# Latent attention on one Trainium2 core: keys and values of two head groups projected ahead of the first queries, a later transposition of probabilities, and shorter weight tiles

## The chip, the cores and the metric

The kernel runs on one core of a Trainium2 chip, as one launch. The metric is the device time of an execution in microseconds, as the median of several runs. TensorE is written PE here, VectorE DVE, ScalarE ACT, GpSimd POOL and SyncE SP.

## What is computed

The reference runs two blocks of two layers each on one sequence of 256 tokens with 1024 features. The first block mixes by forgetting attention, a short convolution and pooling, then by a gated feed-forward layer. In the second block the first layer mixes by latent attention and the second by dilated attention, each followed by a feed-forward layer. The change is in the latent attention, and in numbers that all parts share:

```python
def mla_mixer(h, pos, w_in, g_qa, w_qb, g_kva, w_kvb, g_q, g_k, w_o):
    proj = h @ w_in
    q_lat = proj[..., :Q_LORA]                      # 384
    kv_lat = proj[..., Q_LORA:Q_LORA + KV_LORA]     # 256
    k_rope = rope(proj[..., Q_LORA + KV_LORA:], pos)
    q = (rms_norm(q_lat, g_qa) @ w_qb).reshape(B, S, MLA_HEADS, MLA_QK)
    kv = (rms_norm(kv_lat, g_kva) @ w_kvb).reshape(B, S, MLA_HEADS, MLA_NOPE + MLA_V)
    ...
    q = rms_norm(q, g_q)
    k = rms_norm(k, g_k)
    o = dense_attention(q, k, v, MLA_QK ** -0.5)    # 16 heads, softmax over all 256 keys
    return o.reshape(B, S, MLA_HEADS * MLA_V) @ w_o
```

## The kernel before, in words

**Weights.** `plan()` writes a list of weight chunks in the order of their use. `use(ci)` (from L318) returns the chunk whose turn it is; it starts the DMA of a chunk four ahead into a `raw` tile (SP's queue, L304) and the split of a chunk two ahead. Float32 products are built from two reduced-precision parts: ACT casts the weights to `whi` (L313) and DVE subtracts to get `wlo` (L314). `mm3` then issues three matmuls for one product: L362 to L364 where the weights move through PE, L366 to L368 where they are held. A chunk has at most 2048 floats a partition; `CHUNK` sets only how long the tiles are.

**Order.** The code issues work in program order, and a scheduler (the Tile framework's) decides from it, from its own costs and from free buffers the order on each engine. An engine runs its list strictly in that order. So a row that waits holds up everything below it.

**Latent attention.** The 16 heads are four groups g of four. `lat_proj` and `latent` (L1268 to L1298) make the latents of keys and of queries, normalise them (DVE L1288), transpose them on PE (L1294) and split them for the next product (ACT L474, DVE L475). For a group there are three pieces:

- `proj_kv(g)` (L1319): 12 matmuls of 512 columns into two accumulator banks, then ACT's square (L1330), DVE's sum (L1331) and a copy of the values (L1337). Called kv0 to kv3 below.
- `post_kv(g)` (L1341): DVE writes the scaled keys out of the same two banks (L1345, L1346). Only then are the banks free.
- `proj_q(g)` (L1350): 18 matmuls of 384 columns into two banks, ACT's square (L1360) and copy (L1361), DVE's sum (L1362) and the rotation (L1255 to L1258), which reads the banks too. Called q0 to q3.

There are four accumulator banks in PSUM (`accp`), used by every product, and four other PSUM banks (`attp`) for scores and transposes. `tr_qk(hd)` transposes a head's queries and keys (PE L1374, ACT L1376 and L1377).

`attn_std` (L650) runs the heads as a pipeline: scores of head i (`st0`: PE L674, DVE L677 and L678, ACT's exponential L640, DVE L643 and L648), then the transposition of the probabilities of head i - D1 (`st1`: PE L695, ACT L697), then, for a pair of heads, the product with the values of heads i - D2 (`st2`: PE L707 and L711, split by ACT L479 and DVE L480). `D1, D2` are 3 and 6 for the first block's causal attention and 1 and 4 here. Probabilities and their transposes take tiles of 512 floats from one pool, `t2p`, of five.

A table of due steps calls kv2, q2, kv3, q3 and the heads' `tr_qk` between the heads. From step 23 on, `out_ahead` fills in matmuls of the output projection (L366 to L368), whose weights are split like all others. Beside all that run pieces of the bias of the dilated attention (PE L760 and L762, DVE L744, L769 and L775), fed in by `next(bias)`.

The start of the attention, before:

```python
    proj_kv(0)
    qlT = next(qlT)
    proj_q(0)
    post_kv(0)
    proj_kv(1)
    proj_q(1)
    post_kv(1)
    for hd in range(4):
        tr_qk(hd)
```

`next(qlT)` is the transposition of the latent queries.

Of the kernel before, what the change touches and what calls it, by code (L numbers as in the profile page):

```python
# [55 lines left out]

CHUNK = 2112
LOWP = 100  # L60


def seq_chunks(blocks):

    return [("blk", blocks[i:i + 16]) for i in range(0, len(blocks), 16)]


def plan():
    chunks = []
# [37 lines left out]
        chunks.append(("wide", "mla_w_in_2", 0, k0, 4, [(384, 288)]))  # L107
    for k0 in (0, 4):
        chunks.append(("wide", "mla_w_in_2", 0, k0, 4, [(0, 384)]))
    for g in range(4):  # L110
        kn = [((4 * g + h) * 128, 64) for h in range(4)]
        vv = [((4 * g + h) * 128 + 64, 64) for h in range(4)]
        chunks.append(("wide", "mla_w_kvb_2", 0, 0, 2, kn + vv))
        chunks.append(("wide", "mla_w_qb_2", 0, 0, 3, [(g * 384, 384)]))
    chunks += seq_chunks([("mla_w_o_2", 0, k * 128, m * 128) for m in range(8) for k in range(8)])
    for i in range(2):
        if i == 1:
# [123 lines left out]
def tile_net(ctx, tc, wts, ada, xin, cols_in, table_in, fb_in, c_in, pos_in, inv_in, mask_in, freq_in, out):  # L241
# [6 lines left out]
    rawp = ctx.enter_context(tc.tile_pool(name="rawp", bufs=4))  # L248
    splp = ctx.enter_context(tc.tile_pool(name="splp", bufs=3))
    t1p = ctx.enter_context(tc.tile_pool(name="t1p", bufs=6))  # L250
    t2p = ctx.enter_context(tc.tile_pool(name="t2p", bufs=5))
    smp = ctx.enter_context(tc.tile_pool(name="smp", bufs=14))
    accp = ctx.enter_context(tc.tile_pool(name="accp", bufs=4, space=PS))
    attp = ctx.enter_context(tc.tile_pool(name="attp", bufs=4, space=PS))
# [34 lines left out]


    chunks = plan()
    offs, o = [], 0
    for c in chunks:
# [7 lines left out]
    def w_dma(ci):  # L301
        n = chunk_size(chunks[ci])
        r = mk(rawp, [128, CHUNK], F32, "raw")
        nc.sync.dma_start(out=r[:, :n], in_=wts[offs[ci]:offs[ci] + 128 * n].rearrange("(p f) -> p f", f=n))  # L304
        raw[ci] = r

    def split_piece():
        ci, a, b, last = pend.pop(0)
        if a == 0:
            spl[ci] = (mk(splp, [128, CHUNK], F32R, "whi"), mk(splp, [128, CHUNK], F32R, "wlo"))  # L310
        hi, lo = spl[ci]
# [203 lines left out]
    for _ in range(12):  # L515
        PE.matmul(out=wps[:, :128], lhsT=ones, rhs=ones, start=True, stop=True)
    raw[0] = mk(rawp, [128, CHUNK], F32, "raw")
    w0 = wts[0:128 * 1056].rearrange("(p f) -> p f", f=1056)
# [131 lines left out]
    def attn_std(heads, qkT, vcol, oT, causal, qscale=None, done=set()):  # L650


        P, PT, O = {}, {}, {}
        D1, D2 = (3, 6) if causal else (1, 4)

        def st0(h_):
            qk = qkT(h_)
# [661 lines left out]
    def proj_kv(g):  # L1319
        w = use(nextc())  # L1320
        akv = [acc(), acc()]
        for k in range(2):
            for tt in range(2):
                mm3(akv[tt], w, slice(k * 512, k * 512 + 512), parts(kvT[k], slice(tt * 128, tt * 128 + 128)), k == 0, k == 1, wmov=True, ns=648)
        vt = bt([128, 2, 256])
        vM[g] = vt
        ss = sm(8)
        for tt in range(2):
            sq = t1()
            S.activation(out=sq, in_=akv[tt][:, :256], func=AF.Square)  # L1330
            V.tensor_reduce(out=ss[:, 4 * tt:4 * tt + 4], in_=sq.rearrange("p (a b) -> p a b", a=4), axis=AX.X, op=ALU.add)  # L1331
        V.tensor_tensor(out=ss[:, :8].rearrange("p (t a) -> p t a", t=2), in0=ss[:, :8].rearrange("p (t a) -> p t a", t=2),
                        in1=skr.unsqueeze(2).to_broadcast([128, 2, 4]), op=ALU.add)
        r = sm(8)
        rsqrt_small(r[:, :8], ss[:, :8], 8, 1.0 / 96)
        for tt in range(2):
            S.copy(out=vt[:, tt, :], in_=akv[tt][:, 256:512])  # L1337
        postM[g, 1] = (akv, r)

    def post_kv(g):  # L1340
        akv, r = postM.pop((g, 1))  # L1341
        for tt in range(2):
            rk = r[:, 4 * tt:4 * tt + 4].unsqueeze(2)
            ka = bt([128, 4, 96])
            V.tensor_tensor(out=ka[:, :, 0:64], in0=akv[tt][:, :256].rearrange("p (a b) -> p a b", a=4), in1=rk.to_broadcast([128, 4, 64]), op=ALU.mult)  # L1345
            V.tensor_tensor(out=ka[:, :, 64:96], in0=kr[tt].to_broadcast([128, 4, 32]), in1=rk.to_broadcast([128, 4, 32]), op=ALU.mult)  # L1346
            qaM[g, 1, tt] = ka

    def proj_q(g):
        w = use(nextc())  # L1350
        aq = [acc(), acc()]
        for k in range(3):
            for tt in range(2):
                mm3(aq[tt][:, :384], w, slice(k * 384, k * 384 + 384), parts(qlT[k], slice(tt * 128, tt * 128 + 128)), k == 0, k == 2, wmov=True, ns=490)
        ss = sm(8)
        for tt in range(2):
            qb = bt([128, 4, 96])
            q3 = aq[tt][:, :384].rearrange("p (a b) -> p a b", a=4)
            sq2 = t2()
            S.activation(out=sq2[:, :384], in_=aq[tt][:, :384], func=AF.Square)  # L1360
            S.copy(out=qb[:, :, 0:64], in_=q3[:, :, 0:64])  # L1361
            V.tensor_reduce(out=ss[:, 4 * tt:4 * tt + 4], in_=sq2[:, :384].rearrange("p (a b) -> p a b", a=4), axis=AX.X, op=ALU.add)  # L1362
            rope_to(qb[:, :, 64:96], q3[:, :, 64:96], tt, t1([128, 4, 32]), 4)
            qaM[g, 0, tt] = qb
        r = mk(smp, [128, 8], F32, "rq", 3)
        rsqrt_small(r, ss[:, :8], 8, 1.0 / 96)
        rM[g] = r
# [46 lines left out]
        yield acs  # L1414

    proj_kv(0)
    qlT = next(qlT)
    proj_q(0)
    post_kv(0)
    proj_kv(1)  # L1420
    proj_q(1)
    post_kv(1)
    for hd in range(4):
# [242 lines left out]
```

## Time and profile before

| | |
|---|---|
| median of 3 runs | 1575.88 us (1573.53 to 1576.39) |
| the profiled execution's own time | 1574.72 us |
| its span, first to last instruction | 1573.0 us |
| mean granted clock of PE | 0.999 of full speed |
| busy: PE, DVE, ACT, POOL | 1551.7, 1188.2, 899.7, 227.3 us |
| read from HBM | 311.32 MB, 203 GB/s over the span |

The times in the trace are in microseconds from the start of the span. Busy time of PE is the union of its matmuls; the weight loads (PEld) lie beside them. In a timeline a row gives start, duration, engine, line of the kernel, operation, output and inputs, and in brackets how long the engine stood idle before it and what released it. Durations of neighbouring rows overlap a little, since engines are pipelined.

### The profile page before, as it was taken

Reading aid. Unit: us, or ns where it says so; the run is one execution under the profiler, and the core shown is the slowest. Engines: PE = TensorE matmul, PEld = TensorE weight load, DVE = VectorE, ACT = ScalarE, POOL = GpSimd, SP = SyncE. Lnnn points to the kernel's source line nnn. Section 1 sums busy time; section 2 is a strip of 40 time slices with the busy share of each in tenths; the row PEclk is TensorE's granted clock in tenths of the full one; section 3 lists DMA queues with packets and bytes.
Section 4 is the critical chain, followed back from the end, with each engine's and each line's share of the span. In section 5 each row is a group of like instructions: output and inputs, shape, how many; then the busy total and the mean of one; then the engine's idle time right before and its main releaser. Section 6 shows DMA issues by size and latency. Waiting matters only on the chain.

```text
span 1573.0 us, 31268 instructions
## 1 busy us (share of the span) xinstructions
PE 1551.7 (99%) x12314; PEld 1506.7 (96%) x12314; DVE 1188.2 (76%) x2430; ACT 899.7 (57%) x1854; POOL 227.3 (14%) x273
## 2 busy tenths in 40 slices
PE   8999999999999999999999999999999999999999
PEld 7999999999899999999987899999999999999999
DVE  7877877789787777778788688767777777686642
ACT  7574554433557454443258677533676766677632
POOL 1100100055210010004332100010223222110000
PEclk9999999999999999999999999999999999999999
DMA  8455666645655666664435267776666767655551
GB/s 315 168 188 201 218 240 218 238 170 163 214 195 189 229 222 228 219 241 170 140 116 188 87 238 265 266 284 224 218 218 210 221 199 236 202 200 186 191 198 41
DMA packets 83907, 320.69 MB, mean 204 GB/s; under 512 B 31984, under 2 KB 34816, under 8 KB 58928
## 3 DMA queue, kind: packets, MB, share of 16 engines
q1 hardware_dynamic: 83184, 317.30, 59.0%
q8 instruction: 97, 1.59, 0.4%
q0 software_dynamic: 432, 1.28, 0.3%
q14 instruction: 50, 0.41, 0.1%
q10 hardware_dynamic: 144, 0.11, 0.0%
HBM read 311.32 MB, written 7.34 MB: 203 GB/s over the span
## 4 chain that ended last, share of the span: by engine, by line
PE 91%; DVE 5%; ACT 1%; issue 1%; POOL 1%; DMA 1%; SPq 0%; ACTq 0%; DVEq 0%; POOLq 0%
PE acc L366 22%; PE acc L368 21%; PE acc L367 21%; PE acc L362 6%; PE acc L363 6%; PE acc L364 6%; DVE wlo L314 2%; PE att L760 1%; PE att L1548 1%; POOL sm L405 1%; PE att L1550 1%; PE att L1562 1%; PE acc L707 1%; PE att L674 1%; PE att L1579 1%
## 5 line engine op out<-in xcount | busy, mean ns | idle before, releaser
L314 DVE TENSOR_TENSOR wlo<-raw,whi 128x1024 fp32r<-128x1024 f32 (+2 forms) x508 | 582.6, 1165 | 149.5 <-ACT whi L313 148.5
L313 ACT CAST whi<-raw 128x1024 fp32r<-128x1024 f32 (+2 forms) x508 | 495.5, 1000 | 313.2 <-PE acc L367 187.4
L366 PE MATMUL acc<-b,whi 128*128 128x256 f32 x1744 | 498.5, 286 | 2.3 <-ACT b L479 0.9
L367 PE MATMUL acc<-b,whi 128*128 128x256 f32 x1744 | 490.0, 281 | 0.0
L368 PE MATMUL acc<-b,wlo 128*128 128x256 f32 x1744 | 489.2, 281 | 0.0
L366 PE MATMUL acc<-h,whi 128*128 128x256 f32 (+1 forms) x1216 | 343.1, 282 | 0.8 <-DVE t L1102 0.8
L368 PE MATMUL acc<-h,wlo 128*128 128x256 f32 (+1 forms) x1216 | 342.2, 281 | 0.0
L367 PE MATMUL acc<-h,whi 128*128 128x256 f32 (+1 forms) x1216 | 341.3, 281 | 0.0
L366 PEld LDWEIGHTS acc<-b,whi 128*128 128x128 f32 x1744 | 328.1, 188 | 6.3 <-issue 3.2
L367 PEld LDWEIGHTS acc<-b,whi 128*128 128x128 f32 x1744 | 328.5, 188 | 1.2 <-issue 0.8
L368 PEld LDWEIGHTS acc<-b,wlo 128*128 128x128 f32 x1744 | 328.5, 188 | 0.1
L366 PEld LDWEIGHTS acc<-h,whi 128*128 128x128 f32 x1216 | 229.8, 189 | 0.9 <-issue 0.9
L368 PEld LDWEIGHTS acc<-h,wlo 128*128 128x128 f32 x1216 | 229.1, 188 | 0.0
L367 PEld LDWEIGHTS acc<-h,whi 128*128 128x128 f32 x1216 | 229.0, 188 | 0.0
L362 PE MATMUL acc<-whi,h 128*128 128x384 f32 (+4 forms) x544 | 191.6, 353 | 2.8 <-ACT whi L313 2.8
L363 PE MATMUL acc<-wlo,h 128*128 128x384 f32 (+4 forms) x544 | 183.0, 337 | 0.6 <-DVE wlo L314 0.6
L364 PE MATMUL acc<-whi,h 128*128 128x384 f32 (+4 forms) x544 | 181.6, 336 | 0.0
L405 POOL TENSOR_TENSOR sm<-sm,mhalf 128x4 f32<-128x4 f32 (+3 forms) x72 | 92.0, 1277 | 351.3 <-DVE sm L404 328.1
L623 DVE CUSTOM_DVE_ANT_0 t<-raw,cond,cols 128x1024 bf16<-128x1024 f32 x96 | 121.7, 1279 | 7.5 <-PE att L690 3.4
L362 PEld LDWEIGHTS acc<-whi,h 128*128 128x128 f32 x544 | 102.7, 189 | 6.9 <-ACT whi L313 3.2
L363 PEld LDWEIGHTS acc<-wlo,h 128*128 128x128 f32 x544 | 103.0, 189 | 3.9 <-DVE wlo L314 1.0
L364 PEld LDWEIGHTS acc<-whi,h 128*128 128x128 f32 x544 | 102.0, 188 | 3.2 <-DVE h L1167 0.3
(256 smaller groups left out, 1736.9 us busy)
## 6 DMA issues: line engine op xcount, KB each, us to landing
raw<-in_wts_dram SPq DMA_DIRECT2D x194, 1024.0 KB, 4.8
raw<-in_ada_dram SPq DMA_DIRECT2D x48, 1024.0 KB, 5.0
raw<-in_wts_dram SPq DMA_DIRECT2D x50, 768.0 KB, 4.4
scr<-b SPq DMA_DIRECT2D x48, 128.0 KB, 3.0
b<-scr SPq DMA_DIRECT2D x64, 96.0 KB, 5.4
raw<-in_wts_dram SPq DMA_DIRECT2D x6, 576.0 KB, 3.8
raw<-in_wts_dram SPq DMA_DIRECT2D x6, 512.0 KB, 3.5
raw<-in_wts_dram SPq DMA_DIRECT2D x3, 528.0 KB, 4.2
```

The source lines that it names most:

```text
L313: S.copy(out=hi[:, a:b], in_=r[:, a:b])
L314: V.tensor_tensor(out=lo[:, a:b], in0=r[:, a:b], in1=hi[:, a:b].bitcast(F32), op=ALU.subtract)
L362: PE.matmul(out=o_ap, lhsT=xhi, rhs=whi, start=start, stop=False)
L363: PE.matmul(out=o_ap, lhsT=xhi, rhs=wlo, start=False, stop=False)
L364: PE.matmul(out=o_ap, lhsT=xlo, rhs=whi, start=False, stop=stop)
L366: PE.matmul(out=o_ap, lhsT=whi, rhs=xhi, start=start, stop=False)
L367: PE.matmul(out=o_ap, lhsT=whi, rhs=xlo, start=False, stop=False)
L368: PE.matmul(out=o_ap, lhsT=wlo, rhs=xhi, start=False, stop=stop)
L405: G.tensor_tensor(out=r, in0=v[:, :n], in1=mhalf[:, :n], op=ALU.pow)
L623: V.tensor_tensor_reduce(out=junk, in0=w[:, e * 1024:e * 1024 + 1024], in1=cond, scale=1.0, scalar=col("ada_b", n), op0=ALU.mult, op1=ALU. ...
L674: PE.matmul(out=ps[:, 256 * i:256 * i + 256], lhsT=qk[:, 0, 128 * i:128 * i + 128], rhs=qk[:, 1, :], start=True, stop=True)
L707: PE.matmul(out=o_, lhsT=vcol(h0 + e, 0), rhs=pt[:, 0:256], start=True, stop=False)
```

## The change

Four edits:

- `CHUNK` 2112 becomes 2048.
- Keys and values of the first two groups (eight heads) are projected first, then the latent queries are transposed, then come `post_kv(0)`, q0 and q1. The chunks of weights stand in the same order in the plan: kv0, kv1, q0, q1, kv2, q2, kv3, q3.
- The pool `t2p` has six tiles instead of five.
- In the attention that isn't causal, D1 becomes 2: a head's probabilities are transposed two heads after its scores instead of one.

```diff
-CHUNK = 2112
+CHUNK = 2048
...
+    kvb, qb = [], []
     for g in range(4):
         kn = [((4 * g + h) * 128, 64) for h in range(4)]
         vv = [((4 * g + h) * 128 + 64, 64) for h in range(4)]
-        chunks.append(("wide", "mla_w_kvb_2", 0, 0, 2, kn + vv))
-        chunks.append(("wide", "mla_w_qb_2", 0, 0, 3, [(g * 384, 384)]))
+        kvb.append(("wide", "mla_w_kvb_2", 0, 0, 2, kn + vv))
+        qb.append(("wide", "mla_w_qb_2", 0, 0, 3, [(g * 384, 384)]))
+    chunks += [kvb[0], kvb[1], qb[0], qb[1], kvb[2], qb[2], kvb[3], qb[3]]
...
-    t2p = ctx.enter_context(tc.tile_pool(name="t2p", bufs=5))
+    t2p = ctx.enter_context(tc.tile_pool(name="t2p", bufs=6))
...
-        D1, D2 = (3, 6) if causal else (1, 4)
+        D1, D2 = (3, 6) if causal else (2, 4)
...
     proj_kv(0)
+    proj_kv(1)
     qlT = next(qlT)
+    post_kv(0)
     proj_q(0)
-    post_kv(0)
-    proj_kv(1)
     proj_q(1)
     post_kv(1)
```

Lines of the new file are two higher than before from `plan()` on (L1345 becomes L1347, L1255 becomes L1257, L314 becomes L316). The number of instructions on each engine is the same for all kinds of work.

The first place is PE's list at the start of the attention. `acc` with a number is an accumulator bank's use, `b_10548` and `b_10549` are the latent of keys and values, `b_10670` to `b_10672` that of queries, and `t` is what L1294 (L1296) transposes. Before:

```order
L364 MATMUL acc_10702<-whi_10593,b_10549 128x512
L1294 MATMUL att_10734<-ident,t_10680 128x128 x3
...
L1294 MATMUL att_10744<-ident,t_10689 128x128 x3
L362 MATMUL acc_10756<-whi_10634,b_10670 128x384
...
L364 MATMUL acc_10757<-whi_10634,b_10672 128x384
L362 MATMUL acc_10829<-whi_10706,b_10548 128x512
...
L364 MATMUL acc_10830<-whi_10706,b_10549 128x512
L362 MATMUL acc_10864<-whi_10780,b_10670 128x384
```

After:

```order
L366 MATMUL acc_10702<-whi_10593,b_10549 128x512
L364 MATMUL acc_10736<-whi_10634,b_10548 128x512
...
L366 MATMUL acc_10737<-whi_10634,b_10549 128x512
L1296 MATMUL att_10785<-ident,t_10680 128x128 x3
L1296 MATMUL att_10795<-ident,t_10689 128x128 x3
...
L364 MATMUL acc_10813<-whi_10706,b_10670 128x384
...
L366 MATMUL acc_10814<-whi_10706,b_10672 128x384
L364 MATMUL acc_10864<-whi_10760,b_10670 128x384
```

kv1 moved ahead of the transposes, and q1 now follows q0 directly.

The second place is DVE's list in the same microseconds. `acc_10701` and `acc_10702` are kv0's banks, `acc_10756` and `acc_10813` a bank of q0 before and after. Before:

```order
L769 TENSOR_TENSOR b_9961<-att_10607,b_9329 64x8x8
L314 TENSOR_TENSOR wlo_10781<-raw_10626,whi_10780 128x1152
L475 SCALAR_TENSOR_TENSOR b_10672<-att_10744,cols,b_10672 128x128
L1362 TENSOR_REDUCE sm_10796<-t_10798 128x4
L1255 TENSOR_TENSOR b_10797<-acc_10756,rtab 128x4x32
...
L1345 TENSOR_TENSOR b_10821<-acc_10701,sm_10728 128x4x64
...
L1345 TENSOR_TENSOR b_10824<-acc_10702,sm_10728 128x4x64
L1346 TENSOR_TENSOR b_10824<-kr_10576,sm_10728 128x4x32
L314 TENSOR_TENSOR wlo_10838<-raw_10699,whi_10837 128x1024
```

After:

```order
L771 TENSOR_TENSOR b_9961<-att_10607,b_9329 64x8x8
L316 TENSOR_TENSOR wlo_10761<-raw_10626,whi_10760 128x1152
L1333 TENSOR_REDUCE sm_10771<-t_10772 128x4
...
L477 SCALAR_TENSOR_TENSOR b_10671<-att_10785,cols,b_10671 128x128
L316 TENSOR_TENSOR wlo_10825<-raw_10699,whi_10824 128x1024
...
L477 SCALAR_TENSOR_TENSOR b_10671<-att_10795,cols,b_10671 128x128
L1347 TENSOR_TENSOR b_10805<-acc_10701,sm_10728 128x4x64
...
L1347 TENSOR_TENSOR b_10808<-acc_10702,sm_10728 128x4x64
...
L1257 TENSOR_TENSOR b_10838<-acc_10813,rtab 128x4x32
```

L1347, which frees kv0's banks, stands ahead of the first rotation now, and behind two splits and five L477.

The third place is DVE's list ahead of the rotation of q2, whose banks kv3 takes. `wlo_11241` belongs to the output projection. Before:

```order
L648 TENSOR_SCALAR t_10975<-t_10975,sm_10984 128x256 x2
L1331 TENSOR_REDUCE sm_11030<-t_11034 128x4
L1255 TENSOR_TENSOR b_11071<-acc_11046,rtab 128x4x32
...
L314 TENSOR_TENSOR wlo_11241<-raw_10995,whi_11240 128x1024
```

After:

```order
L650 TENSOR_SCALAR t_10975<-t_10975,sm_10984 128x256 x2
...
L316 TENSOR_TENSOR wlo_11241<-raw_11003,whi_11240 128x1024 x2
...
L650 TENSOR_SCALAR t_10990<-t_10990,sm_10999 128x256 x2
L1333 TENSOR_REDUCE sm_11038<-t_11042 128x4
L1257 TENSOR_TENSOR b_11079<-acc_11054,rtab 128x4x32
```

Both pieces of that split, and the scaling of a third head's probabilities, now stand ahead of the rotation.

## Rows read from the trace of the kernel before

**Rows 1.** The page: busy us, share of the span and instructions by engine.

```profile
PE 1551.7 (99%) x12314; PEld 1506.7 (96%) x12314; DVE 1188.2 (76%) x2430; ACT 899.7 (57%) x1854; POOL 227.3 (14%) x273
```

**Rows 2.** Busy time in stretches: from:to, length, engines (instructions), PE's clock, DMA share, GB/s.

```profile
65.00:120.00 55.00, 55.00 (x462) 52.84 (x461) 44.88 (x119) 38.77 (x97) 0.45 (x4) 1.00 0.48 173
420.00:780.00 360.00, 360.00 (x3042) 353.92 (x3040) 281.55 (x553) 177.22 (x297) 45.71 (x48) 1.00 0.58 204
...
806.00:839.00 33.00, 29.68 (x165) 24.22 (x163) 29.39 (x97) 24.85 (x62) 10.24 (x8) 1.00 0.64 200
839.00:892.00 53.00, 49.91 (x309) 37.78 (x310) 37.20 (x113) 40.26 (x115) 4.91 (x3) 1.00 0.28 98
```

**Rows 3.** Timeline of PE at the start of the latent attention.

```profile
809.79 0.49 PE L1294 MATMUL att<-ident,t 128*128 128x128 f32 x3
...
811.24 0.55 PE L1294 MATMUL att<-ident,t 128*128 128x128 f32 x3 [0.63 <-DVE t L1288]
...
816.59 0.44 PE L364 MATMUL acc<-whi,b 128*128 128x384 f32 x1 [1.16 <-DVE b L475]
817.60 0.47 PE L362 MATMUL acc<-whi,b 128*128 128x512 f32 x1 [0.57 <-DVE t L1257]
...
820.48 0.34 PE L362 MATMUL acc<-whi,b 128*128 128x384 f32 x1
...
823.62 1.47 PE L1374 MATMUL att<-ident,b 128*96 128x128 f32 x12
...
838.99 0.47 PE L362 MATMUL acc<-whi,b 128*128 128x512 f32 x1 [0.40 <-DVE sm L404]
```

**Rows 4.** Timeline of DVE in the same microseconds.

```profile
811.10 0.41 DVE L1331 TENSOR_REDUCE sm<-t 128x4 f32<-128x256 f32 x1
811.43 0.34 DVE L475 SCALAR_TENSOR_TENSOR b<-att,cols,b 128x128 fp32r<-128x128 f32 x1
...
811.76 0.48 DVE L744 SCALAR_TENSOR_TENSOR oh<-posq,pk,t 128x256 bf16<-128x256 f32 x1
...
812.23 0.59 DVE L769 TENSOR_TENSOR b<-att,b 128x64 f32<-128x64 f32 x3
...
814.79 1.36 DVE L314 TENSOR_TENSOR wlo<-raw,whi 128x1152 fp32r<-128x1152 f32 x1
...
818.85 0.42 DVE L1345 TENSOR_TENSOR b<-acc,sm 128x256 f32<-128x256 f32 x1
...
820.12 1.22 DVE L314 TENSOR_TENSOR wlo<-raw,whi 128x1024 fp32r<-128x1024 f32 x1
```

**Rows 5.** Timeline of PE in the attention proper: transposes and scores that wait.

```profile
847.32 0.30 PE L695 MATMUL att<-ident,t 128*128 128x128 f32 x1 [0.34 <-DVE t L648]
...
850.66 0.30 PE L695 MATMUL att<-ident,t 128*128 128x128 f32 x1 [1.41 <-ACT b L1377]
...
858.02 1.13 PE L674 MATMUL att<-b 96*128 96x256 f32 x4 [0.34 <-ACT t L640]
```

**Rows 6.** Timeline of DVE there: scaling of probabilities, two splits.

```profile
842.57 0.60 DVE L648 TENSOR_SCALAR t<-t,sm 128x256 f32<-128x256 f32 x2
...
843.16 2.35 DVE L314 TENSOR_TENSOR wlo<-raw,whi 128x1024 fp32r<-128x1024 f32 x2
```

**Rows 7.** Timeline of ACT: evacuation of a bank of q0, two casts.

```profile
815.07 0.49 ACT L1360 ACTIVATE t<-acc 128x384 f32<-128x384 f32 x1 [0.31 <-PE acc L364]
815.46 0.37 ACT L1361 COPY b<-acc 128x256 f32<-128x256 f32 x1
...
836.42 2.04 ACT L313 CAST whi<-raw 128x1024 fp32r<-128x1024 f32 x2
```

**Rows 8.** Busy time in stretches of 2 us, columns as in the second group.

```profile
786.00:788.00 2.00, 1.13 (x11) 0.99 (x11) 1.19 (x3) 0.00 (x0) 1.23 (x1) 1.00 0.00 0
788.00:790.00 2.00, 1.81 (x12) 1.81 (x13) 1.06 (x3) 0.55 (x2) 0.14 (x1) 0.75 0.00 0
790.00:792.00 2.00, 2.00 (x11) 1.93 (x11) 2.00 (x6) 0.94 (x3) 0.00 (x0) 0.50 0.00 0
```

## The prediction

> **What bounds the kernel now.** The first view is the busy time by engine: TensorE (PE) is busy 1551.7 of 1573.0 us [rows 1], so a change gains only where PE stands idle, and costs only where it makes PE idle or slow its clock. The second view, busy time in stretches, tells where that is. Outside the latent attention PE has no gap: 55.00 of 55.00 us in a stretch of the first layer, 360.00 of 360.00 in a later one [rows 2]. In the latent attention it has: 29.68 of 33.00 us while the first two head groups are projected, 49.91 of 53.00 us in the attention proper [rows 2]. So the third view is PE's timeline there, read for the idle time in brackets and its releaser [rows 3], and the fourth the queue of VectorE (DVE) in the same microseconds [rows 4]. PE and DVE run in program order, so each row waits for all rows above it.
>
> What the reader is to see in [rows 3]: kv0 (keys and values of heads 0 to 3) is followed at 809.79 by the transposition of the latent queries. PE waits 0.63 us for its second half, 1.16 us for the split of the transposed latent (L475), and 0.57 us until q0's banks are read by the rotation (L1257). Then kv1 runs from 817.60 to 820.48 and q1 from 820.48 to 823.62, that is 12 matmuls in 2.88 us and 18 in 3.14 us, without a gap. Three waits, 2.36 us, are what the new order can hope for here.
>
> **The change, part by part.**
>
> *Chunk size 2048.* No chunk is larger than 2048 floats, so only the tiles' size falls, no row of any engine. Cost 0, with no cover needed.
>
> *Order kv0, kv1, qlT, post_kv(0), q0, q1.* kv1's 2.88 us now run before the transposes, over the wait for the second latent half. That 0.63 us goes. But there are four accumulator banks. kv0 holds two until post_kv(0) has read them (L1345), kv1 takes the other two, and so q0 must wait for L1345. On DVE's order L1345 now stands behind this, counted in the order and priced from [rows 4]: L744 0.48, six L769 in two lots of 0.59, the 1152-float split 1.36, two L1331 at 0.41, five L475 at 0.34 and the 1024-float split 1.22. The sum is 0.48 + 1.18 + 1.36 + 0.82 + 1.70 + 1.22 = 6.76 us. In the rows an instruction starts up to 0.1 us before the one ahead has ended, so I take 6.3. DVE reaches L744 at 811.7 as before; L1345 (0.42) ends near 811.7 + 6.3 + 0.4 = 818.4. PE meanwhile has done kv1 (809.8 + 2.9, with a few bias matmuls, 813.3) and the transposes (814.2). It then idles some **4.2 us**, where before it idled 2.4 in three pieces. q0 takes 3.14 us and a little for its second bank, to 821.9; in the trace before both kv1 and q0 were done at 820.48, so this is +1.4.
>
> q1 now follows q0 at once and takes q0's banks, which are free only after the square, the copy and the rotation. kv1 stood in that gap before (0.57 us after a shorter queue, then 2.88 us of work ahead of q1). Now both of q0's banks fill together, so both stand to be read when q1 comes: on ACT a square (0.49) and a copy (0.37) for each [rows 7], 0.86 us for one bank and 1.72 for both, and the rotation on DVE beside the second. The bounds are 0.57, as in the row, and 1.7; I take 1.4, nearer to the full evacuation, since PE's order fills the two banks in turns. Transposes of the first heads thus start near 826.4 where they started at 823.62: **+2.8**. Nothing is to be caught up behind that, as PE is in order.
>
> By the row of 0.57 us alone q0 and q1 would wait 1.1 us together, and the sum below would be some 3 us smaller. The Trainium skill (Perfetto Trace Analysis, Matmuls under Optimizing Tensor Performance) says that independent matmul groups should rotate through different PSUM banks, so that the evacuation of one overlaps the next one's matmuls. By that rule the new order is the worse one: kv0, q0, kv1, q1 puts another group between every two that share banks, and kv0, kv1, q0, q1 leaves each q's evacuation bare, which is the sum as I make it.
>
> *Lag of two heads.* Transposes of probabilities (L695) come a head later, so the waits on their own softmax go: 0.34 at 847.32, 1.41 at 850.66, 0.34 at 858.02 [rows 5], **-2.1**. The wait of 0.40 before kv3 [rows 3] is replaced. On DVE's order q2's rotation (L1257 in the new file, first of a kind on which kv3's bank depends) now stands behind two 1024-float splits of the output weights, which stood behind it before, and behind one more head's scaling. The rows are 2.35 us for two splits and 0.60 us for L648 [rows 6]: together **+3.0**. Below, 0: q2's own matmuls could end as late as that. Above, 5.0: on ACT two casts of 2.04 us [rows 7] move ahead of the exponential and the copy that the first product with the values needs. I take the rows of DVE, since q2's rotation is the one that kv3 waits for.
>
> *Sixth t2 tile.* It feeds the extra lag. It also lets the scheduler put some softmax steps of the first block's two causal attentions ahead of weight splits. PE is gapless there [rows 2], and a chunk is split two chunks before use; so 0, and if that cover is gone about one split, 1.2 us [rows 4], in each layer.
>
> *The clock.* Around 786 PE was busy only 1.13 of 2 us; the granted clock was 0.75 and 0.50 of full speed in the two following stretches of 2 us [rows 8], that is partly 1.2 GHz instead of 2.4. That cost (0.25 + 0.50) x 2 = 1.5 us. In 806 to 839, with 3.3 us idle in small pieces, it stayed 1.00 [rows 2]. A hole of 4.2 us in one piece is nearer to the first. I take **+1.5**, between 0 and 3.0 (once more before kv3).
>
> The Trainium skill (TensorE: Matmul & The Clock Gate, HAM oscillation) says that idle gaps between bursts of matmuls bring TensorE back to half rate, each time anew. By that rule the second hole counts too and the sum would be 1.5 higher; the row of 806 to 839, where the clock stayed at 1.00 through waits of 1.2 us, speaks against it, so that it stands in the range and in a rival only.
>
> **Sum:** 2.8 + 3.0 + 1.5 - 2.1 = **+5.2 us** on the profiled execution's 1574.72, 1579.9. The median of the runs lies 1.16 above that execution, so I forecast **1581.1 us** against 1575.88. Here 0.2% is 3.15 us, about what a measurement of this kernel can tell from no change.
>
> **Rivals.**
>
> *A: faster, the latent-query wait is covered and nothing replaces it.* If post_kv(0) gets its turn on DVE by about 814.2, when the transposes end, q0 finds its banks free. For it: kv0's reduction is done at 811.5, and L1345 itself is only 0.42 us. Against it: the 6.3 us of queue above it, the two splits foremost; the point is whether these are finished 4 us earlier than I add up. Then the 2.36 us go, the lag brings 2.1, and kv3's delay of 3.0 hides behind q2: 1574.72 - 4.5 + 1.16 = **1571.4**.
>
> *B: no change that can be measured.* The hole exists, yet the bias matmuls that fall into it hold the clock at 1.00, and the splits ahead of q2's rotation run while PE still works on q2. Then only 2.8 - 2.1 = +0.7 is left: **1576.6**. For it: the 1.00 in 806 to 839 with 10% idle [rows 2], and PE's 3.1 us of idle time in the 53 us after that, which can absorb something. Against it: two casts and two splits in a row ahead of one rotation.
>
> *C: slower still.* PE's clock falls a second time: 1581.1 + 1.5 = **1582.6**. If the lag brings nothing as well, because the transposes then wait for the next head's exponential in the same ACT queue, 1584.7.
>
> **How the numbers follow.** Forecast and C together 0.55 (0.40 and 0.15), B 0.28, A 0.17. The range goes from A's 1571.4, with a little for the spread of runs, to C with no gain from the lag, with as much above: **1571.0 to 1586.0**; slower cases alone give 1579 to 1586. Faster 0.17, same 0.28, slower 0.55. A's weight reflects that all of the hole rests on one queue, which I added up from rows of another order.
>
> **What would show it right or wrong.** In the profile after, PE's timeline should have one idle piece of about 4 us right after the latent queries' transposes, released by DVE L1347 (L1345 before), a second of about 1.4 us before q1, and a third of 2 to 3 us before kv3, released by the rotation or by ACT's L697. The granted clock should be below 1.00 in the stretches after the first. The transposes of probabilities should show hardly a wait on DVE's scaling. The stretches 65 to 120 and 420 to 780 should stay gapless. The prediction is wrong if L1347 of group 0 is done within a microsecond of the transposes' end, if the clock stays 1.00 in the whole attention, or if the stretch from kv0's end to the first full column block of the output projection (839 to 892 before, [rows 2]) is no longer than before.

## The result and the profile after

The changed kernel took **1586.03 us** (median of 4 runs, 1583.23 to 1586.92) against 1575.54 us for the kernel before in the same comparison. The ratio on record is 1.0064, with a 95% interval of 1.0052 to 1.0076: slower by 10.5 us by the medians, by 8 to 12 us by the interval. The profiled execution took 1583.23 us, with a span of 1581.5 us.

The page, busy time by engine, against [rows 1]:

```profile
PE 1555.4 (98%) x12314; PEld 1510.2 (95%) x12314; DVE 1188.8 (75%) x2430; ACT 900.7 (57%) x1854; POOL 228.1 (14%) x273
```

PE has the same 12314 matmuls and is busy 3.7 us longer, which is matmuls at a lower clock; the other 4.8 us of the longer span are idle. The busy time in stretches (from:to, length, engines, PE's clock, DMA share, GB/s), first those of [rows 2], then pieces of 2 us:

```profile
65.00:120.00 55.00, 55.00 (x462) 52.86 (x460) 45.48 (x118) 39.12 (x98) 0.45 (x4) 1.00 0.49 172
420.00:780.00 360.00, 360.00 (x3045) 354.08 (x3044) 281.97 (x554) 177.58 (x297) 45.70 (x48) 1.00 0.58 204
806.00:839.00 33.00, 27.13 (x147) 23.36 (x145) 26.31 (x81) 21.09 (x53) 9.09 (x6) 0.95 0.57 175
839.00:892.00 53.00, 46.12 (x256) 33.93 (x257) 35.78 (x115) 37.84 (x109) 6.54 (x4) 0.94 0.30 102
816.00:818.00 2.00, 1.64 (x5) 1.67 (x6) 1.87 (x7) 0.28 (x1) 0.00 (x0) 0.55 0.81 209
818.00:820.00 2.00, 2.00 (x8) 2.00 (x8) 0.00 (x0) 0.00 (x0) 0.00 (x0) 0.60 0.98 396
844.00:846.00 2.00, 1.97 (x5) 1.59 (x6) 1.98 (x8) 0.97 (x3) 1.68 (x2) 0.50 0.85 336
846.00:848.00 2.00, 2.00 (x9) 1.58 (x7) 0.78 (x3) 1.61 (x6) 0.00 (x0) 0.77 0.07 27
864.00:866.00 2.00, 2.00 (x8) 0.92 (x7) 2.00 (x5) 1.05 (x4) 0.00 (x0) 0.50 0.00 0
866.00:868.00 2.00, 2.00 (x9) 1.74 (x9) 1.16 (x2) 1.04 (x3) 0.00 (x0) 0.65 0.00 0
```

The stretches of the first block are as gapless as before. In the latent attention PE is idle 5.9 us in the first stretch (3.3 before) and 6.9 us in the second (3.1 before), and the clock, 1.00 before, is 0.95 and 0.94. It falls three times: after 816, by 844 and after 864. Before the attention this execution happened to be 2.2 us early (kv0 starts at 804.75, at 806.99 before): 0.8 us of that stood already at 786, and for the rest the fall of the clock of [rows 8] is missing in it (1.00 from 786 to 794, after the same two waits of 1.04 and 1.06 us). So from kv0 to the end it lost 8.5 + 2.2 = 10.7 us.

PE's timeline, the waits that count:

```profile
811.18 0.81 PE L1296 MATMUL att<-ident,t 128*128 128x128 f32 x6
...
816.36 0.66 PE L364 MATMUL acc<-whi,b 128*128 128x384 f32 x1 [4.19 <-ACT b L476]
...
822.43 0.42 PE L364 MATMUL acc<-whi,b 128*128 128x384 f32 x1 [1.20 <-DVE t L1259]
...
840.02 0.64 PE L1376 MATMUL att<-ident,b 128*96 128x128 f32 x4 [1.23 <-ACT t L642]
842.54 0.62 PE L709 MATMUL acc<-t,b 128*64 128x256 f32 x2 [1.87 <-DVE t L1259]
844.03 0.79 PE L364 MATMUL acc<-whi,b 128*128 128x512 f32 x1 [0.87 <-DVE t L1259]
...
863.36 0.64 PE L1376 MATMUL att<-ident,b 128*96 128x128 f32 x4 [2.59 <-ACT t L642]
```

Against [rows 3] and [rows 5]: the transposes of both latent halves now run in one piece at 811.18, with no wait for the second half. Then there is a hole of 4.19 us ahead of q0 and one of 1.20 us ahead of q1. The waits of 1.23, 1.87 and 0.87 us stand ahead of a q/k transpose, of the first product with the values and of kv3, where 0.40 us stood before kv3 and another 0.40 us three microseconds ahead of it, which [rows 3] leaves out. PE's timeline, before:

```profile
836.09 0.30 PE L695 MATMUL att<-ident,t 128*128 128x128 f32 x1 [0.40 <-DVE t L648]
```

The old waits of 0.34 and 1.41 us in the attention proper are gone, but one of 2.59 us is new, for ACT's exponential.

DVE's timeline over the first hole:

```profile
813.43 0.35 DVE L477 SCALAR_TENSOR_TENSOR b<-att,cols,b 128x128 fp32r<-128x128 f32 x1
...
814.15 1.22 DVE L316 TENSOR_TENSOR wlo<-raw,whi 128x1024 fp32r<-128x1024 f32 x1
...
815.80 0.41 DVE L1347 TENSOR_TENSOR b<-acc,sm 128x256 f32<-128x256 f32 x1
```

L1347, the scaling that frees a bank of kv0, starts at 815.80 and ends at 816.21; q0 starts at 816.36. The page names ACT's L476 as the releaser, which ended at about the same time, but q0's first matmul reads the latent part whose splits were through by 813.8 (second L477). The bank is what it waits for, which the third experiment tests.

DVE's and ACT's timelines over the other two:

```profile
838.18 2.36 DVE L316 TENSOR_TENSOR wlo<-raw,whi 128x1024 fp32r<-128x1024 f32 x2
...
840.84 0.61 DVE L650 TENSOR_SCALAR t<-t,sm 128x256 f32<-128x256 f32 x2
...
842.17 0.22 DVE L1259 TENSOR_TENSOR t<-acc,rtab 128x64 f32<-128x64 f32 x1
...
861.06 0.68 DVE L679 TENSOR_REDUCE sm<-att 128x2 f32<-128x512 f32 x1
```

```profile
836.88 1.99 ACT L315 CAST whi<-raw 128x1024 fp32r<-128x1024 f32 x2 [0.39 <-ACT t L642]
838.77 0.56 ACT L642 ACTIVATE t<-att,sm,rq 128x256 f32<-128x256 f32 x1
...
859.14 2.04 ACT L315 CAST whi<-raw 128x1024 fp32r<-128x1024 f32 x2
...
862.11 0.56 ACT L642 ACTIVATE t<-att,sm,rq 128x256 f32<-128x256 f32 x1 [0.65 <-DVE sm L680]
```

On ACT two casts of the output weights, 1.99 us, stand ahead of the third head's exponential (838.77). DVE runs the two splits from 838.18, scales that head at 840.84 and only then reaches q2's rotation, whose last step on the first bank ends at 842.39. The first product with the values, which takes that bank, starts at 842.54. The wait of 1.23 us is of another kind: the q/k transposes at 840.02 start 0.14 us after the third head's exponential ends on ACT (839.88), and need the bank that its scores held. In the later wait the head's maximum (L679) is taken at 861.06 behind q3's evacuation on DVE, its exponential follows at 862.11, and at 863.36 PE goes on with a transpose that has nothing to do with that head. What it needs is a bank for its output. The four banks of scores and transposes hold the scores written from 855.34 and from 858.73, the transposes from 857.86 and the q/k transposes from 858.29. None of the four is emptied before that exponential ends at 863.21.

### The profile page after: what moved, and what is told of

Its sections match the earlier page's. It is cut to its first block, busy times and chain, and to the rows that moved or that the text cites. A ratio compares the mean times of both kernels' runs of the same rounds, so it can differ in the third digit from the quotient of the medians.

```text
span 1581.5 us, 31277 instructions
## 1 busy us (share of the span) xinstructions
PE 1555.4 (98%) x12314; PEld 1510.2 (95%) x12314; DVE 1188.8 (75%) x2430; ACT 900.7 (57%) x1854; POOL 228.1 (14%) x273
## 4 chain that ended last, share of the span: by engine, by line
PE 91%; DVE 5%; issue 1%; ACT 1%; POOL 1%; DMA 1%; SPq 0%; ACTq 0%; DVEq 0%; POOLq 0%
PE acc L368 22%; PE acc L370 21%; PE acc L369 21%; PE acc L364 6%; PE acc L366 6%; PE acc L365 6%; DVE wlo L316 2%; PE att L762 1%; PE att L1550 1%; POOL sm L407 1%; PE att L1552 1%; PE acc L709 1%; PE att L1564 1%; PE att L676 1%; PE att L1581 1%
## 5 line engine op out<-in xcount | busy, mean ns | idle before, releaser
L316 DVE TENSOR_TENSOR wlo<-raw,whi 128x1024 fp32r<-128x1024 f32 (+2 forms) x508 | 582.5, 1165 | 146.5 <-ACT whi L315 145.5
```

Source lines behind the costliest of these rows:

```text
L316: V.tensor_tensor(out=lo[:, a:b], in0=r[:, a:b], in1=hi[:, a:b].bitcast(F32), op=ALU.subtract)
```

## The experiments

Ratios are estimates on record from all executions of a kernel and of the kernel before, run on the same chip in turns, with 95% intervals. They can differ from the quotient of the medians by up to 0.0006. Three groups of experiments ran on three chips, so that across groups only the ratios are compared. Lines in a kernel whose plan is unchanged are those of before; otherwise they are shifted by 2 to 8.

**The order alone** (`e_order`).

```diff
-CHUNK = 2112
+CHUNK = 2048
...
+    chunks += [kvb[0], kvb[1], qb[0], qb[1], kvb[2], qb[2], kvb[3], qb[3]]
...
     proj_kv(0)
+    proj_kv(1)
     qlT = next(qlT)
+    post_kv(0)
     proj_q(0)
-    post_kv(0)
-    proj_kv(1)
```

Expected:

> Only the order of the projections and of their weight chunks is changed (and the chunk size), the lag stays 1 and the pool stays at five tiles. Theory A, two causes that add: the new order pays the 4.19 us hole ahead of q0, the 1.20 us ahead of q1 and one fall of the clock (about 1.7), and saves the three waits of 2.36 us, so +4.7: about 1580.2 us; kv3's banks are read in time, as before, and the attention proper shows the old waits (0.3 to 1.4 us). Rival B, the order is the cause of all: the late start moves the whole attention out of step, and the time is that of the full change, about 1586. Rival C, the order costs nothing by itself, since later idle time takes it up: within 2 us of 1575.5.

Measured: 1578.29 us, ratio 1.0017 (1.0006 to 1.0029). PE's timeline:

```profile
820.72 0.66 PE L364 MATMUL acc<-whi,b 128*128 128x384 f32 x1 [4.19 <-ACT b L476]
...
827.57 0.41 PE L364 MATMUL acc<-whi,b 128*128 128x384 f32 x1 [1.15 <-DVE t L1259]
```

Both holes are there with the same length as in the full change (4.19 and 1.15), and the attention proper shows the old waits (0.30, 0.35, 1.41). So theory A has the mechanism, and B falls. The size is nearer to 2.7 than to 4.7 us (0.9 to 4.6 us by the interval): the idle time alone accounts for 4.19 + 1.15 + 0.34 - 2.36 = 3.3 us, where 0.34 is a small wait inside kv1, released by L1290. The fall of the clock, which I had counted as new, also occurs in some executions of the old order (below); that this is why the size is less is not shown. The interval doesn't exclude C's two microseconds either, but its reason isn't seen: nothing later takes the holes up in the timeline.

**The lag alone** (`e_lag`), with the sixth tile and the shorter weight tiles:

```diff
-        D1, D2 = (3, 6) if causal else (1, 4)
+        D1, D2 = (3, 6) if causal else (2, 4)
...
-    t2p = ctx.enter_context(tc.tile_pool(name="t2p", bufs=5))
+    t2p = ctx.enter_context(tc.tile_pool(name="t2p", bufs=6))
```

> Only the lag of two heads is changed, with the sixth tile that it needs (and the chunk size); the projections stand in the old order. Theory A: the waits ahead of the first product with the values and of kv3 (3.97 us where 0.40 stood) and the late wait for the exponential (2.59 us where 2.1 us of waits stood) remain, with two falls of the clock of about 1.7 each: +3.6 +0.8 +3.4 less what other waits give back, about +6 to +7, 1581.5 to 1582.5 us, with the three waits of 2.36 us ahead as in the kernel before. Rival B, the order is the cause of all: within 2 us of 1575.5. Rival C, the lag is the cause of all: about 1586.

Measured: 1582.77 us, ratio 1.0044 (1.0031 to 1.0057). PE's timeline:

```profile
837.99 0.64 PE L1374 MATMUL att<-ident,b 128*96 128x128 f32 x4 [0.82 <-ACT t L640]
840.91 1.09 PE L707 MATMUL acc<-t,b 128*64 128x256 f32 x2 [2.28 <-DVE t L1257]
...
862.65 0.64 PE L1374 MATMUL att<-ident,b 128*96 128x128 f32 x4 [2.58 <-ACT t L640]
```

The waits of the lag are all there without the new order; two more, of 0.61 and 0.40 us, stand beside the first two. The two parts add: 1.0017 and 1.0044 make 1.0061, the full change has 1.0064. Theory A holds, and the lag is the larger part. Its two falls of the clock do not both show: after the gap of 2.58 us the clock stayed at 1.00 in this execution, where the full change had 0.50:

```profile
864.00:866.00 2.00, 2.00 (x12) 1.30 (x11) 2.00 (x4) 1.37 (x4) 0.00 (x0) 1.00 0.00 0
```

**The keys scaled early** (`e_order_early`), the full change with one line moved:

```diff
     proj_kv(1)
+    post_kv(0)
     qlT = next(qlT)
-    post_kv(0)
     proj_q(0)
```

> The full change, but the scaling of the first group's keys, which frees the two banks that q0 takes, is written ahead of the transposition of the latent queries, and so stands ahead of the splits of that latent and of the 1024-float weight split in VectorE's list. Theory A, the hole waits for the banks: q0 starts about 2 us earlier in relation to the transposes (then it waits for the split of the latent), so 2 us less, or 3.7 with no fall of the clock there: 1582.3 to 1584 us. Rival B, the hole waits for the split of the latent: q0 starts no earlier, or later by the 1.3 us that the scaling takes: 1586 to 1587.

Measured: 1583.13 us, ratio 1.0048 (1.0034 to 1.0062). PE's timeline, DVE's release of the first bank, and the stretches of 2 us around q0:

```profile
813.91 0.41 PE L364 MATMUL acc<-whi,b 128*128 128x384 f32 x1 [1.50 <-DVE sm L1334]
...
819.90 0.41 PE L364 MATMUL acc<-whi,b 128*128 128x384 f32 x1 [1.54 <-DVE t L1259]
```

```profile
813.34 0.42 DVE L1347 TENSOR_TENSOR b<-acc,sm 128x256 f32<-128x256 f32 x1
```

```profile
814.00:816.00 2.00, 1.90 (x9) 1.44 (x10) 2.00 (x7) 0.62 (x2) 1.64 (x1) 1.00 0.67 258
816.00:818.00 2.00, 1.75 (x10) 1.36 (x9) 2.00 (x7) 0.62 (x2) 0.00 (x0) 1.00 0.48 70
```

The hole of 4.19 us becomes 1.50, the clock stays at 1.00, and the time falls by 2.9 us by the medians, by 2.5 by the ratios, between A's 2 and 3.7 us (the intervals of the two ratios overlap a little). The hole was a wait for banks. What is left of it is one still: L1347 ends at 813.76 and q0 starts at 813.91, ahead of the last L476 of the latent (816.60), so that L476, which the page names in the full change, can't have held q0 up. The wait ahead of q1, whose banks are q0's still, stays (1.54).

**The hole filled** (`e_fill`), the full change with matmuls that nobody reads; their result is no part of the output:

```diff
     post_kv(0)
+    pd = att()
+    for _ in range(34):
+        PE.matmul(out=pd[:, :256], lhsT=parts(kvT[0], slice(0, 128))[0], rhs=parts(kvT[1], slice(0, 256))[0], start=True, stop=True)
     proj_q(0)
```

> The full change, with 34 matmuls of 256 columns between the transposes of the latent queries and q0, into a bank that nobody reads; they take 34 x 0.117 = 4.0 us of the 4.19 us hole. Theory A, the hole costs its own length and a fall of the clock besides: the clock stays at 1.00 through q0 and the run is 1.5 to 1.7 us shorter than the full change, about 1584.4 us. Rival B, the low clock of q0 costs nothing that shows in the end: 1586.0, or more by what the extra matmuls hold up.

Measured: 1584.26 us, ratio 1.0054 (1.0042 to 1.0067). PE's timeline and one stretch:

```profile
813.14 4.22 PE L1424 MATMUL att<-b,b 128*128 128x256 f32 x34
...
817.76 0.41 PE L364 MATMUL acc<-whi,b 128*128 128x384 f32 x1 [0.21 <-ACT b L476]
```

```profile
818.00:820.00 2.00, 2.00 (x13) 2.00 (x13) 1.27 (x5) 0.00 (x0) 0.00 (x0) 1.00 0.68 266
```

q0 starts no earlier after the transposes, but runs at a clock of 1.00, where the full change had 0.55 and 0.60. The medians lie 1.8 us apart, the ratios 1.6, as theory A has it; the intervals overlap, so that the gain in time isn't shown by this run alone. What is shown is the clock in the two profiles, with the lengths of q0's matmuls.

**The split held back** (`e_lag_dep`), the lag alone with a cast that reads a column that holds 1.0 and is written from q2's rotated queries (`wo0` is the first chunk of the output weights):

```diff
-        S.copy(out=hi[:, a:b], in_=r[:, a:b])
+        if ci == wo0:
+            S.activation(out=hi[:, a:b], in_=r[:, a:b], func=AF.Copy, scale=gate[0][:, 0:1])
+        else:
+            S.copy(out=hi[:, a:b], in_=r[:, a:b])
...
             qaM[g, 0, tt] = qb
+            if g == 2 and tt == 1:
+                gate.append(mk(smp, [128, 1], F32, "gate", 1))
+                V.tensor_scalar(out=gate[0][:, 0:1], in0=qb[:, 0, 64:65], scalar1=0.0, scalar2=1.0, op0=ALU.mult, op1=ALU.add)
```

> The lag of two heads in the old order of projections, as in the run before, but the cast of the first chunk of output weights is scaled by a column that VectorE sets to 1.0 from q2's rotated queries, so that this cast, and with it the split, comes behind q2's rotation. Nothing else is moved. Theory A, the wait ahead of the first values and of kv3 comes from that chunk: its two casts (2.0 us) stand ahead of the third head's exponential, whose result VectorE scales ahead of q2's rotation. Then the waits of 0.61, 0.82, 2.28 and 0.40 us shrink from 4.1 to about 1 us and the clock stays at 1.00 there: 3 to 4.8 us less than the lag alone, 1578 to 1580 us. The late wait of 2.6 us remains. Rival B, the lag itself does it (the values come two heads after the scores whatever stands between): 1582 to 1584 us, the waits as before.

Measured: 1586.17 us, ratio 1.0061 (1.0045 to 1.0076). PE's timeline:

```profile
837.09 1.09 PE L712 MATMUL acc<-t,b 128*64 128x256 f32 x2 [1.43 <-DVE t L1262]
...
857.44 1.12 PE L712 MATMUL acc<-t,b 128*64 128x256 f32 x4 [2.22 <-DVE t L1262]
...
860.98 1.09 PE L1382 MATMUL att<-ident,b 128*96 128x128 f32 x4 [1.57 <-ACT t L645]
```

DVE's, ahead of the third head's scaling:

```profile
835.00 0.17 DVE L648 RECIPROCAL sm<-sm 128x2 f32<-128x2 f32 x1 [1.35 <-ACT t L645]
```

A miss. The wait ahead of the first values shrinks by 0.85 us only (2.28 to 1.43), and the 0.60, 0.84 and 0.40 us beside it stay. With the split gone, DVE stands idle for 1.35 us until ACT's exponential of the third head is through, so that two chains of nearly the same length end at that scaling. The held-back work then meets q3's evacuation: 2.22 and 1.57 us where 2.58 and 0.45 stood, and the whole is 2.7 us slower than the lag alone by the ratios (the intervals overlap). So the split of the output weights was a part of the delay and not its cause.

**The due steps one earlier** (`e_lag_shift`), the lag alone with:

```diff
-        todo += [(8 * g + n_, f) for n_, f in ops]
+        todo += [(8 * g + n_ - 1, f) for n_, f in ops]
```

> The lag of two heads in the old order of projections, with every due step of the projections and of the q/k transposes one step earlier (1 in place of 2, 4 in place of 5, and so on in each group). With lag 1 the steps before q2 are the scores of heads 0 and 1; with lag 2 at the same number they are the scores of heads 0, 1 and 2, so that one more head's softmax stands ahead of q2's rotation on VectorE and ScalarE. One step earlier, the scores of two heads stand ahead of q2 again. Theory A, the waits of the lag are those of a table that was counted for lag 1: the waits of 0.82, 2.28 and 0.40 us ahead of the first values and of kv3 and the late one of 2.6 us fall to below 1 us each and the clock stays at 1.00 there: 5 to 8 us less than the lag alone (1582.8), 1575 to 1578 us, or below the kernel before if the old waits of 0.34 and 1.41 us go as well. Rival B, the lag itself is too long for four banks of scores: the scores' banks are still held when the next ones are due, waits of 2 us and more remain, 1581 to 1584 us.

Measured: 1580.88 us, ratio 1.0030 (1.0019 to 1.0042). PE's, DVE's and ACT's timelines:

```profile
844.73 1.12 PE L695 MATMUL att<-ident,t 128*128 128x128 f32 x4 [4.40 <-ACT t L640]
```

```profile
842.21 0.21 DVE L1257 TENSOR_TENSOR t<-acc,rtab 128x64 f32<-128x64 f32 x1
...
842.41 0.68 DVE L677 TENSOR_REDUCE sm<-att 128x2 f32<-128x512 f32 x1
```

```profile
843.48 0.56 ACT L640 ACTIVATE t<-att,sm,rq 128x256 f32<-128x256 f32 x1 [1.92 <-DVE sm L678]
```

The waits ahead of the first values and of kv3 are gone, as A says, and one of 4.40 us stands in their place. The transpose of head 1's probabilities needs one of the four banks of scores and transposes. The one that comes free next holds head 2's scores, whose maximum (L677) now stands behind q2's rotation (L1257) on DVE and whose exponential follows at 843.48. During the wait all four are held, by the scores of heads 2 and 3 (PE from 837.57 and 838.87), the transposes of head 0 (838.43) and those of a later head's queries and keys (839.73). The probabilities that the transpose reads were ready by 839.78. That is B's mechanism. The late wait is 1.75 us, above the 1 us that A had. About 2 us are won by the ratios, 1.0044 to 1.0030; the intervals overlap.

**Keys of both groups early** (`e_post`), the order of the change with lag 1:

```diff
     proj_kv(0)
+    proj_kv(1)
+    post_kv(0)
     qlT = next(qlT)
+    post_kv(1)
     proj_q(0)
-    post_kv(0)
-    proj_kv(1)
     proj_q(1)
-    post_kv(1)
```

> The new order of the projections with lag 1 and five tiles, but the scaling of the first group's keys is written ahead of the transposition of the latent queries and that of the second group's keys ahead of q0. Then q0 takes banks that are free early and q1 takes kv1's instead of q0's. Theory A, both holes are waits for banks: q0 waits 1.5 to 2 us for the split of the latent in place of 4.19 us and with no fall of the clock, q1 waits 0 to 0.5 us in place of 1.15: 3 to 4.5 us less than the new order alone (1578.3), so 1573.8 to 1575.3, at or just below the kernel before. Rival B, the early scalings only shift VectorE's work and delay the splits: 1577 to 1579 us.

Measured: 1574.89 us, ratio 0.9990 (0.9979 to 1.0000). PE's timeline:

```profile
815.18 0.41 PE L364 MATMUL acc<-whi,b 128*128 128x384 f32 x1 [1.50 <-DVE sm L1334]
...
817.88 0.71 PE L366 MATMUL acc<-whi,b 128*128 128x384 f32 x2 [0.25 <-DVE b L477]
```

q0 waits 1.50 us in place of 4.19, then 0.25 inside, and there is no wait ahead of q1, which now takes kv1's banks. Against the order alone, 1.0017, that is 4.3 us by the ratios, as theory A has it: both holes were waits for banks, and with the banks freed earlier the new order costs nothing. As in the run before with early scaling, the 1.50 us are still the bank's: L1347 ends at 815.03.

**Both mended** (`e_post_lag`): `e_post` with lag 2, six tiles and the due steps one earlier.

> The full change mended in both places: early scalings of both groups' keys, and the due steps one earlier. Theory A, the two mendings add: the order gives 1 to 2 us below the kernel before (as measured alone), the lag with shifted steps 0 to 2 us more: 1572 to 1575 us. Rival B, the lag costs by itself: above 1578 us.

Measured: 1578.99 us, ratio 1.0018 (1.0006 to 1.0029). Theory B: the lag costs some 4 us against `e_post` even so, and the intervals do not overlap. PE's timeline has a wait of 4.12 us for the exponential of a later head and one of 1.74.

**Idle matmuls ahead of the attention** (`e_warm`), the kernel before with:

```diff
-            keep_warm((4, 7)[i])
+            keep_warm((7, 7)[i])
             nrm.part1()
-            keep_warm((2, 2)[i])
+            keep_warm((5, 2)[i])
```

> The kernel before with three more idle matmuls on ones in each of the two waits of about 1.05 us ahead of the latent attention (around 786 us in the trace of before, where the clock fell). Theory A, two short waits close together cost a fall of the clock in most executions: the clock stays at 1.00 from 784 to 796 us, 1 to 2 us less than before, 1574 us or so. Rival B, the extra matmuls hold up the norm's own by as much as the clock gives back: within 0.7 us of before.

Measured: 1577.01 us, ratio 1.0006 (0.9994 to 1.0017), no change that can be told. Two stretches of 2 us, as in [rows 8]:

```profile
788.00:790.00 2.00, 1.52 (x14) 1.46 (x14) 1.48 (x3) 0.19 (x1) 0.49 (x1) 1.00 0.31 29
790.00:792.00 2.00, 2.00 (x19) 1.99 (x18) 2.00 (x6) 1.12 (x3) 0.00 (x0) 1.00 0.60 233
```

The clock stayed at 1.00 there in this execution, and the time shows no gain. The other profiles tell why little was to be had: in eleven the two waits of 1.04 and 1.06 us are as in the kernel before, and only in three (the kernel before, `e_order`, `e_lag_shift`) did the clock fall after them. So the fall is no rule, and theory A's "in most executions" is not borne out. Rival B's time came out, within 0.7 us by the medians; whether for its reason, that the extra matmuls hold up the norm, stays open.

**A version meant to beat both** (`e_best`): `e_post` with those idle matmuls.

> The order with early scalings of keys and the extra idle matmuls together. Theory A of both runs, added: 2 to 4 us below the kernel before, 1572 to 1574 us. Rival: no more than the better of the two alone.

Measured: 1575.27 us where the kernel before had 1576.91, ratio 0.9986 (0.9975 to 0.9997). It is faster than the kernel before by a little, less than the 2 to 4 us of theory A by the medians, and not to be told from `e_post`, as the rival has it.

**Tiles alone** (`e_chunk_t2`): weight tiles of 2048 floats and six t2 tiles, nothing else.

> Only the shorter weight tiles and the sixth t2 tile. Both theories: no change, within 1.5 us of the kernel before; PE without gaps from 65 to 120 and from 420 to 780 us although softmax steps of the first block's attentions come ahead of weight splits there. A rival: the splits come late in that block, 1 us or more in each of its layers, 1577 to 1579 us.

Measured: 1575.01 us, ratio 0.9994 (0.9985 to 1.0003). Three stretches:

```profile
65.00:120.00 55.00, 55.00 (x462) 52.86 (x461) 45.45 (x119) 38.47 (x97) 0.45 (x4) 1.00 0.49 167
420.00:780.00 360.00, 360.00 (x3034) 353.74 (x3034) 281.83 (x554) 178.68 (x299) 45.70 (x48) 1.00 0.59 205
818.00:820.00 2.00, 2.00 (x7) 1.54 (x6) 2.00 (x10) 1.05 (x3) 1.40 (x1) 0.59 0.42 168
```

No change, with PE gapless where the softmax steps moved. The third stretch is the old order's kv1 with the clock at 0.59, after waits of 1.16 and 0.57 us; in the profile of before the same stretch had 1.00.

## Why the prediction came out as it did

It gave slower, 1581.1 us, +5.2. Slower is right; the effect was twice what was forecast. The time of 1586.03 lies 0.03 us above the end of the range, and 1575.88 times the ratio of 1.0064 just inside it. That it comes so near the range is owed to rival C's numbers, which set that end and had a chance of 0.15, and not to the sum, which had half of the loss. By its own steps:

- *Chunk size and sixth tile, 0.* Right: 0.9994 with both.
- *The hole ahead of q0, 4.2 us, from one queue on DVE.* Right, and for the reason given: 4.19 us, DVE's queue from L746 (809.45) to the end of L1347 took 6.76 us where 6.7 were added up, and moving L1347 up shortened the hole to 1.50.
- *The wait ahead of q1, 1.4 us.* Right: 1.20.
- *The order in all, 2.8, and 1.5 for the clock.* More than the 2.7 us measured with the clock in it, though the interval (0.9 to 4.6) still holds the 4.3. The old order's waits cost a fall of the clock as well in some executions, so the new one's is not all new.
- *The wait ahead of kv3, +3.0.* The place and about the size are right: 1.87 + 0.87 = 2.74 us for the banks that q2's rotation frees, beside 1.23 us for a bank of scores, where 0.40 and 0.40 stood. Its cause was given as two splits and one scaling ahead of the rotation on DVE, and in the profile after DVE has no gap there. But the run with the split held back won 0.85 us of it only, since DVE then waits 1.35 us for ACT's exponential. What decides is that a third head's softmax stands ahead; with the due steps one earlier this wait went and another took its place.
- *The lag's gain, -2.1.* This is the step that failed. The three waits did go, but 2.59 and 0.32 us came in their place (a transpose that waits for a bank held by a later head's scores), so that -2.1 became +0.8, and two more falls of the clock came with the lag's waits. The lag alone costs 6.9 us where the prediction had 3.0 - 2.1 = 0.9. The rows had been misread: all three were taken for waits of a transpose on its own softmax, and only 0.34 at 847.32 names DVE's scaling. The wait of 1.41 names ACT's L1377, which empties a bank of q/k transposes (the scaling, L648 at 850.17, was through hardly earlier), and the one at 858.02 is of scores (L674) released by an exponential. So the banks of scores and transposes were short in [rows 5] already. That the transposes would wait for the next head's exponential stood in rival C, as a part of its upper end, at 0.15 with the second fall of the clock.
- *The clock, +1.5 for one fall.* In the profile after there are three. In the first, eight matmuls of q0 took 1.15 us more than at full speed; in the second, six of kv3 took 2.72 us (844.03 to 846.75) where 0.24 each, as in [rows 3], makes 1.4. Reckoned as the prediction did, the three pairs of stretches above make 1.7 + 1.5 + 1.7 = 4.9 us, an upper estimate, as PE was idle in a part of them. The rule of the Trainium skill (TensorE: Matmul & The Clock Gate, HAM oscillation) that was weighed against the row of 806 to 839, and left to the range, agrees with the profile after: each of its three groups of gaps is followed by a stretch at about half the clock. `e_lag` doesn't agree throughout: after its gap of 2.58 us the clock stayed at 1.00.
- *The bank rule.* The Trainium skill (Perfetto Trace Analysis, Matmuls under Optimizing Tensor Performance) was taken to speak against the order kv0, kv1, q0, q1. The trace agrees for the code as changed, but the order itself was not at fault: with both key scalings early the same order of matmuls is at 0.9990.

Rival A (faster, the bank freed in time) did not come true in the change, but its condition was the right one to name. `e_post` comes nearer to it without fulfilling it: the transposes end at 813.5 and L1347 only at 815.03. Its waits of 0.32, 1.50 and 0.25 us stand in for the three of 2.36 us, which saves 0.3 us; its ratio gives 1.6 us (0 to 3.3), and what the rest of that is, if it is more than noise, is not shown. Rival B fell with the clock.

Left open: that the waits of 2.59 and 4.40 us are for banks of scores rests on the timelines, by the count of banks above and by the start of the waiting transposes 0.15 us after a later head's exponential ends, of which they read nothing. A kernel with a fifth such bank was not tried.

## What to carry to other kernels

Before moving a product ahead of another, find which buffer the later one inherits and where, in the order of the engine that frees it, that release stands; here moving two lines of program order turned a loss of 2.7 us into no loss. A longer lag in a software pipeline puts one more stage's work ahead of everything due at a fixed step and, by the timelines here, lets one more stage's scores take a bank first; so the waits that it removes are to be weighed against those at the next shared buffer. Before counting a wait as saved, look whether its releaser is the engine that makes the data or the one that empties a bank. A hole in an engine's queue costs more than its length where the clock falls after it.

## What was not expected of the hardware

In the profile after, the clock of TensorE fell after each long gap or group of gaps, to 0.55 and 0.60, to 0.50 and 0.77, and to 0.50 and 0.65 of full speed in stretches of 2 us. In the first, eight matmuls of 384 columns took 2.56 us (816.82 to 819.38), where eight of the same took 1.41 us at full speed (820.48 to 821.89 in the trace of before). Filling the gap kept it at 1.00. In the old order the stretch after waits of 1.16 and 0.57 us had 1.00 in the profile of before and 0.59 in that of the kernel with other tiles, whose PE order there is the same: the same gaps cost a fall in one execution and none in another. The times of one kernel follow this: of 27 executions of the kernel before beside `e_lag_shift`, `e_post_lag` and `e_chunk_t2`, the fastest (1572.29 us) had a mean granted clock of 1.000 and the slowest (1581.54 us) 0.994. So a part of the spread between executions goes with the clock and not with the code.
